# Second projection of an FFN: a join one step later on ScalarE, an update of x one step later on VectorE

## The chip, the cores and the metric

The kernel runs on one core of one Trainium2 chip. The metric is the device time of one execution in microseconds, as a median over runs. Five engines work side by side, each through its own list of instructions in order, and wait for one another through semaphores: TensorE (PE; its weight loads are shown apart as PEld), VectorE (DVE), ScalarE (ACT), GpSimd (POOL) and SyncE (SP), whose queue issues most of the transfers.

## The reference

The kernel computes an encoder trunk of two layers on one sequence of 512 tokens with 1024 channels, in float32. Cut to its frame:

```python
def swiglu(x, w_in, w_out):
    gu = x @ w_in
    g, u = jnp.split(gu, 2, axis=-1)
    return (jax.nn.silu(g) * u) @ w_out

for l in range(DEPTH):                      # DEPTH = 2
    x = x + 0.5 * swiglu(rms_norm(x, ffn1_norm[l]), ffn1_w_in[l], ffn1_w_out[l])
    x = x + mixer(rms_norm(x, mix_norm[l]), ...)
    x = x + 0.5 * swiglu(rms_norm(x, ffn2_norm[l]), ffn2_w_in[l], ffn2_w_out[l])
return rms_norm(x, final_norm)
```

The hidden width of an FFN is 2816. There are four FFN stages, two in each layer, with a mixer (neighbourhood attention and a Fourier mix) between the two of a layer. The change touches the second projection of the four FFN stages, `(silu(g) * u) @ w_out`, and the addition to x that follows it.

## The kernel before

**Products in parts.** Matrix products run in float32r, with each operand split into a high part (ACT copies it into the narrower format) and a low part (DVE subtracts). A product is then three matmuls: high by high, low by high, high by low. A weight comes from memory as `raw` and becomes `whi` (ACT, L191 or L186) and `wlo` (DVE, L194 or L187); some are first added to another block by DVE (`summed`, L164). `whi` and `wlo` have three buffers each. `ws.next()` hands out the next weight and prepares those up to two ahead (`AHEAD`).

**Seven products.** Each large product is a two by two block product done with seven products in the manner of Strassen, numbered 1 to 7. In the second projection the blocks of the result are quarters of x, written `(i, j)`: `i` is the half of the channels, `j` the half of the tokens. Several products serve more than one quarter: product 1 is accumulated in the bank pair `ps[1]`, is subtracted from quarter (0, 0), then product 6 is accumulated on top of it in the same pair (`key = {6: 1, 4: 7}`), and the sum of products 1 and 6 goes into (1, 1), (0, 1) and (1, 0).

**The steps.** The inner dimension is cut in three chunks, `c` = 0, 1, 2. A list of 21 steps (L758 to L769) sets the order on TensorE: steps 0 to 2 are product 1 with chunks 0 to 2, steps 3 to 5 product 2, steps 6 to 17 products 5, 6, 7, 3 for chunk 0, then for chunk 1, then for chunk 2, and steps 18 to 20 product 4. `make(i)` (L772) prepares the activations of step i: some add or subtract two blocks first (`comb`, DVE L750), then ACT splits off the high part (`c1h`, `c2h`, ..., L321) and DVE the low part (`c1l`, `c2l`, ..., L322); the digit is the product. The loop at L920 makes a step's activations one or two steps ahead, issues its matmuls, and then whatever stands behind the step.

**Turned halves.** The activations `silu(g) * u` come out of the first projection with tokens on the partitions and must be transposed. `halves` (L693) has ACT separate the two 16-bit words of each number (`apart`, L341; tiles `zs`) and SP issue a transposing transfer (`zt<-zs`, L347). `joined` (L697) has ACT put the words together again in the tile `at` (L356, two ACT instructions a half here). When the second projection begins, two halves of the last block of four feature tiles are still to be joined: those of the second token half, turned first, and those of the first token half, turned last. `turned.reverse()` at step 2 takes the last one first. It is the block `at[1, 0, 2]`, chunk 2 of product 2, so step 5 is the first to read it. The other is `at[1, 1, 2]`; it is joined behind step 5 and first read for chunk 2 of products 6, 7 and 3.

**Updates of x.** `update(ps, i, j, sign)` (L753) adds a pair of banks to a quarter of x, in two DVE instructions (L756). Where a quarter is done, ACT squares it for the next norm (`squares`, L375), and TensorE transposes it for the next stage (`quad`, L402, matmuls at L413 into `tr`). Behind step 18 quarters (1, 1) and (0, 1) are transposed in three of the four stages; the last stage (`late`) goes on to the final norm instead.

**What sets the order.** TensorE's work, ACT's and DVE's is ordered by a planner when the program is built: it goes by the order in which the program writes the instructions, but lets one pass whose inputs and buffers it reckons ready earlier. Inside a `manual_schedule` block the written order holds for the engines named; the block behind step 18 is one, for DVE and ACT. The planner's reckoning is not the chip's time, so an instruction can stand early in an engine's list and wait there, and all behind it wait too.

Of the kernel before, what the change touches and what calls it, by code (L numbers as in the profile page):

```python
# [90 lines left out]
def encoder_kernel(  # L91
# [19 lines left out]
    def slot(dt=F32, s="k", shape=(4, 256)):  # L111
        return kp.tile([P, *shape], dt, tag="k", name=nm(s), bufs=23)
# [8 lines left out]
    def pair(s="ps"):  # L121
        return [bank(s), bank(s)]
# [149 lines left out]
    class Stream:  # L272
# [32 lines left out]
        def next(self, ahead=AHEAD):  # L305
            self.prep(self.pos + 1 + ahead)
            it = self.items[self.pos]
            self.pos += 1
            return it.out
# [203 lines left out]
    def product(ps, acts, kts, start, stop=True, again=False, hook=None, by_block=False, ahead=AHEAD):  # L513

        h, l, off = acts
        n = (len(kts) + 1) // 2

        def granule(i, w, b):  # L520
            res = []
            for k, kt in enumerate(kts[2 * i : 2 * i + 2]):
                c, z = slice(off + b * P, off + (b + 1) * P), slice(k * T, (k + 1) * T)
                res.append((
                    ps[b], h[:, kt, c], l[:, kt, c], w[0][:, z], w[1][:, z], start and i + k == 0,
                    stop and 2 * i + k == len(kts) - 1,
                ))
            return res

        if by_block:  # L530
            w = [ws.next() for _ in range(n)]
            for b in range(2):
                for i in range(n):
                    late_low(granule(i, w[i], b), again)
            return
        for i in range(n):
            w = ws.next(AHEAD if i < n - 1 and ahead else ahead)
            if i < n - 1:
                late_low(granule(i, w, 0) + granule(i, w, 1), again)
            else:  # L540
                late_low(granule(i, w, 0), again)
                late_low(granule(i, w, 1), again)
            if hook and i == 0:
                hook()
# [70 lines left out]
    def stage_ffn(norm, nxt, late):  # L615
# [81 lines left out]
        def joined():  # L697

            t, j, f0 = turned.pop(0)
            q = 0  # L700
            while q < 4:
                h, c, i = PLACE[f0 + q]
                n = 1
                while q + n < 4 and PLACE[f0 + q + n] == (h, c, i + n):
                    n += 1
                joined_words(at_tile(h, j, c)[:, i : i + n, :], t[:, :, q : q + n, :])
                q += n
# [14 lines left out]
        def settle_at():  # L722
            while late_at:
                to_at(*late_at.pop(0))
# [28 lines left out]
        def update(ps, i, j, sign, bs=(0, 1)):  # L753
            for b in bs:
                v = x[:, 2 * j + b, i * T : (i + 1) * T]
                V.scalar_tensor_tensor(v, ps[b], 0.25 * sign, v, ALU.mult, ALU.add)  # L756
# [15 lines left out]
        def make(i):  # L772
            if i < len(steps) and i not in made:
                m, c, f = steps[i]
                made[i] = hl(f(), c, f"c{m}")
# [144 lines left out]
        for i, (m, c, _) in enumerate(steps):  # L920
            make(i)
            if i:
                make(i + 1)
            key = {6: 1, 4: 7}.get(m, m)
            if key not in ps:
                ps[key] = pair(f"o{key}")
            if m == 4 and c == 0 and nxt.mix:
                make(i + 2)
                ws.finish_stage()
                swap_pools(1)  # L930
            product(
                ps[key], made.pop(i), list(range(len(CHUNK[0][c]))), c == 0 and m in (1, 2, 3, 5, 7), c == 2,
                m in (4, 6), by_block=late and i == len(steps) - 1,
            )
            if i == 0:
                settle_at()
            if i == 2:
                turned.reverse()
                joined()
            if i == 5:  # L940
                joined()
            if m == 4 and c == 0 and not late:
                with tc.manual_schedule(engines={mybir.EngineType.DVE, mybir.EngineType.Activation}):
                    make(i + 2)
                    nxt.quad(1, 1)
                    if nxt.mix:
                        nxt.low01 = nxt.quad_high(0, 1)
                    else:
                        nxt.quad(0, 1)
            make(i + 2)  # L950
            if i == 6 and not late:
                nxt.quad(0, 0)
            if m == 4 and c == 1:
                update(ps[1], 1, 0, 1)
            if m == 4 and c == 0 and late:
                gf[0] = slot(F32, "gf", (D,))
                nc.sync.dma_start(out=gf[0], in_=bass.AP(tensor=gfin.tensor, offset=gfin.offset, ap=[[0, P], [1, D]]))
            if c < 2:
                continue
            if m == 1:  # L960
                update(ps[1], 0, 0, -1)
            elif m == 2:
                update(ps[2], 0, 0, 1)
                nxt.squares(0, 0)
            elif m == 5:
                update(ps[5], 0, 1, 1)
                update(ps[5], 1, 1, -1)
            elif m == 6:
                update(ps[1], 1, 1, 1)
            elif m == 7:  # L970
                update(ps[7], 1, 1, 1)
                nxt.squares(1, 1)
                update(ps[1], 0, 1, -1)
            elif m == 3:
                update(ps[3], 0, 1, 1)
                nxt.squares(0, 1)
                if late:
                    make(i + 3)
            elif late:
                with (  # L980
                    tc.issue_after(ws.items[-1].last.ins),
                    tc.manual_schedule(engines={mybir.EngineType.DVE, mybir.EngineType.Activation}),
                ):
                    ready = nxt.inverses(2)
                    next(ready)
                    gained(2, 0)
                    next(ready)
                    gained(2, 1)
                    for _ in ready:
                        pass  # L990
                    scaled(nxt, 2)
                    update(ps[7], 1, 0, 1, (0,))
                    nxt.squares(1, 0, (0,))
                    root = [nxt.inverse(b, *nxt.terms(b)) for b in range(2)]
                    next(root[0])
                    gained(3, 0)
                    gained(3, 1)
                    scaled(nxt, 3)
                    update(ps[7], 1, 0, 1, (1,))
                    nxt.squares(1, 0, (1,))  # L1000
                    next(root[1])
                    next(root[0])
                    gained(0, 0)
                    next(root[0])
                    gained(0, 1)
                    scaled(nxt, 0)
                    next(root[1])
                    next(root[1])
                    whole(nxt, 1, 0)
                    whole(nxt, 1, 1)  # L1010
            else:
                update(ps[7], 1, 0, 1)
                if not nxt.mix:
                    nxt.squares(1, 0)
                nxt.later((1, 0))
# [8 lines left out]
    def gained(tb, i):  # L1024

        if tb not in ob:
            ob[tb] = slot(F32, "o", (D,))
        o_, v, g, _ = half(tb, i)
        V.tensor_tensor(o_, v, g, ALU.mult)

    def scaled(norm, tb):

        o_, _, _, to = half(tb)
        S.activation(o_, o_, AF.Copy, scale=norm.inv[tb])
        nc.sync.dma_start(out=to, in_=o_)

    def whole(norm, tb, i):
        if tb not in ob:
            ob[tb] = slot(F32, "o", (D,))
        o_, v, g, to = half(tb, i)  # L1040
        V.scalar_tensor_tensor(o_, v, norm.inv[tb], g, ALU.mult, ALU.mult)
        nc.sync.dma_start(out=to, in_=o_)
# [770 lines left out]
    def swap_pools(kind, fetch=True):  # L1813

        if scope[0]:
            scope[0].close()
        scope[0] = ExitStack()
        name = nm("stage")
        scope_pool[0] = scope[0].enter_context(tc.tile_pool(name=name, bufs=1, reuse_waits="tile"))
        if kind:  # L1820
            mix_pool[0] = scope_pool[0]
            raw_pool[0] = mix_raw
        else:
            raw_pool[0] = ffn_raw
        if fetch:
            ws.enter(ws.stage + 1)
# [163 lines left out]
```

## Time and profile before

| | |
|---|---|
| median of 3 runs | 1859.08 us (1858.87 to 1861.8) |
| profiled execution, whole | 1858.25 us |
| its span, first to last instruction | 1856.5 us |
| granted TensorE clock, mean | 0.998 of full speed |
| second projections of the four FFN stages (first step to last) | from about 220, 821, 1143 and 1742 us, some 110 us each |

Busy times and waits stand in the rows that the prediction shows. Times in a timeline are microseconds from the start of the span. A row of the timeline gives start, duration, engine, line, operation and the tiles written and read; in brackets stands how long the engine had idled before it and what ended that. A row of the list of waits reads "engine, tile and line that waited <- what it waited for: total us, number, longest". A TensorE matmul's end is modelled, so the starts of its weight loads (PEld) show best where it stood still.

### The profile page before, as it was taken

What the parts mean: (1) busy time and instruction counts of PE and PEld (TensorE: products, weight loads), DVE (VectorE), ACT (ScalarE), POOL (GpSimd) and SP (SyncE); (2) the same over time, 40 slices, a digit from 0 to 9 for tenths busy, and PEclk for the clock granted to TensorE, in tenths of its full rate; (3) what the DMA queues carried; (4) which work ended last, traced back from release to release, by engine and by line L of the source; (5) the groups of instructions that cost most, each with busy time, mean ns of one, the idle gap of its engine ahead of it and who ended that gap; (6) DMA issues with size and microseconds to landing.
All of it is one profiled execution on the core that took longest, in us unless ns stands there. A gap on an engine that the chain in (4) does not pass through costs nothing.

```text
span 1856.5 us, 24608 instructions
## 1 busy us (share of the span) xinstructions
PE 1842.9 (99%) x8862; PEld 1529.9 (82%) x8862; DVE 1605.1 (86%) x1950; ACT 1311.4 (71%) x1780; POOL 171.4 (9%) x210
## 2 busy tenths in 40 slices
PE   9999999999999999999999999999999999999998
PEld 7888888888888888888788888888888888888886
DVE  7878899786989987889998888998869899888898
ACT  6777875668676767777666777766675776777865
POOL 0001011100111010001010100101001101010010
PEclk9999999999999999999999999999999999999999
DMA  9898798932896788979888887989249867888794
GB/s 302 227 234 220 189 262 271 221 114 91 246 232 180 182 225 221 213 199 260 250 199 220 223 210 207 270 274 215 74 143 237 230 179 174 232 212 209 218 283 146
DMA packets 198458, 394.21 MB, mean 212 GB/s; under 512 B 103808, under 2 KB 103936, under 8 KB 198336
## 3 DMA queue, kind: packets, MB, share of 16 engines
q1 hardware_dynamic: 169664, 294.30, 49.4%
q0 software_dynamic: 28528, 98.33, 29.8%
q8 instruction: 69, 1.13, 0.3%
q14 instruction: 53, 0.43, 0.1%
q10 hardware_dynamic: 144, 0.02, 0.0%
HBM read 365.85 MB, written 2.11 MB: 198 GB/s over the span
## 4 chain that ended last, share of the span: by engine, by line
PE 89%; DVE 5%; issue 2%; DMA 2%; ACT 1%; SPq 0%; DVEq 0%; ACTq 0%
PE A L508 10%; PE A L511 10%; PE A L509 10%; PE B L509 5%; PE B L508 5%; PE B L511 5%; PE o L511 5%; PE o L508 5%; PE o L509 5%; PE ps L315 4%; PE ps L316 3%; PE ps L317 3%; PE C L508 3%; PE C L509 3%; PE C L511 3%
## 5 line engine op out<-in xcount | busy, mean ns | idle before, releaser
L194 DVE TENSOR_TENSOR wlo<-raw,whi 128x1024 fp32r<-128x1024 f32 (+1 forms) x534 | 630.2, 1190 | 165.2 <-ACT whi L191 163.7
L191 ACT ACTIVATE whi<-raw 128x1024 fp32r<-128x1024 f32 (+1 forms) x534 | 545.8, 1033 | 250.9 <-DVE raw L164 57.5
L150 POOL DMA_DIRECT2D raw<-in_wst_dram x166 | 144.3, 886 | 1343.1 <-DMA raw<-in_wst_dram 812.7
L164 DVE TENSOR_TENSOR raw<-raw,raw 128x1024 f32<-128x1024 f32 (+1 forms) x150 | 178.5, 1190 | 2.0
L509 PE MATMUL A<-whi,xl 128*128 128x512 f32 x400 | 155.7, 389 | 0.0
L508 PE MATMUL A<-whi,xh 128*128 128x512 f32 x400 | 155.7, 389 | 0.0
L356 ACT ACTIVATE at<-zt 128x1024 uint16<-128x1024 uint16 (+2 forms) x96 | 110.4, 1167 | 22.4 <-DMA zt<-zs 22.4
L186 ACT ACTIVATE whi<-raw 128x1024 fp32r<-128x1024 f32 (+1 forms) x83 | 86.0, 1036 | 46.6 <-issue 12.5
L511 PE MATMUL A<-wlo,xh 128*128 128x512 f32 x400 | 115.0, 389 | 0.0
L187 DVE SCALAR_TENSOR_TENSOR wlo<-raw,whi 128x1024 fp32r<-128x1024 f32 (+1 forms) x83 | 98.2, 1192 | 11.2 <-ACT whi L186 11.2
L511 PEld LDWEIGHTS A<-wlo,xh 128*128 128x128 f32 x400 | 75.1, 188 | 15.6
L509 PEld LDWEIGHTS A<-whi,xl 128*128 128x128 f32 x400 | 75.1, 188 | 15.4
L508 PEld LDWEIGHTS A<-whi,xh 128*128 128x128 f32 x400 | 75.1, 188 | 15.4
L508 PE MATMUL C<-whi,xh 128*128 128x512 f32 x208 | 81.1, 390 | 0.0
L509 PE MATMUL C<-whi,xl 128*128 128x512 f32 x208 | 81.0, 389 | 0.0
L509 PE MATMUL B<-whi,xl 128*128 128x512 f32 x208 | 81.0, 389 | 0.0
L508 PE MATMUL B<-whi,xh 128*128 128x512 f32 x208 | 80.9, 389 | 0.0
L346 ACT ACTIVATE zs<-th 128x1024 uint16<-128x1024 uint16 x80 | 79.5, 1041 | 0.9 <-DVE th L737 0.9
L730 ACT ACTIVATE th<-sn,rh 128x512 f32<-128x512 f32 x80 | 55.1, 716 | 34.0 <-DVE sn L583 33.0
L578 ACT ACTIVATE sn<-A 128x512 f32<-128x512 f32 x104 | 59.1, 585 | 24.8 <-PE A L511 24.8
L511 PE MATMUL C<-wlo,xh 128*128 128x512 f32 x208 | 59.8, 389 | 0.0
L511 PE MATMUL B<-wlo,xh 128*128 128x512 f32 x208 | 59.8, 389 | 0.0
(438 smaller groups left out, 4680.2 us busy)
## 6 DMA issues: line engine op xcount, KB each, us to landing
raw<-in_wst_dram SPq DMA_DIRECT2D x470, 512.0 KB, 5.7
raw<-in_wst_dram POOLq DMA_DIRECT2D x174, 512.0 KB, 7.8
raw<-in_wst_dram SPq DMA_DIRECT2D x30, 256.0 KB, 4.0
bm<-in_bias_dram SPq DMA_DIRECT2D x16, 384.0 KB, 3.6
x<-in_xin_dram SPq DMA_DIRECT2D x4, 512.0 KB, 10.2
raw<-in_wst_dram POOLq DMA_DIRECT2D x8, 256.0 KB, 9.2
dft<-in_dft_dram POOLq DMA_DIRECT2D x8, 256.0 KB, 4.3
gb<-in_gbias_dram SPq DMA_DIRECT2D x4, 512.0 KB, 15.2
```

The lines of the kernel that those rows point to most:

```text
L150: G.dma_start(out=self.t, in_=wst[GRAN_AT[self.plus]][:, 0 : self.n], accum_op=ALU.add)
L164: V.tensor_tensor(self.raw.t, self.raw.t, self.add.t, ALU.add)
L186: S.activation(hi, t, AF.Copy, scale=-1.0)
L187: self.last = V.scalar_tensor_tensor(lo, t, -1.0, hi.bitcast(F32), ALU.mult, ALU.subtract)
L191: S.activation(hi[:, cs], t[:, cs], AF.Copy)
L194: self.last = V.tensor_tensor(lo[:, cs], t[:, cs], hi[:, cs].bitcast(F32), ALU.subtract)
L315: PE.matmul(ps, lh, rh, start=start, stop=False, skip_group_check=again)
L346: S.activation(s[:, h], words[:, h], AF.Copy)
L356: S.activation(to[:, w], t[:, w], AF.Copy)
L508: PE.matmul(ps, lh, rh, start=start, stop=False, skip_group_check=again)
L509: PE.matmul(ps, ll, rh, start=False, stop=False, skip_group_check=again)
L511: PE.matmul(ps, lh, rl, start=False, stop=stop, skip_group_check=again)
```

## The change

Two pieces of work are written one step later in the loop over the 21 steps; nothing else differs.

- The joining of the last turned half, two ACT instructions in each FFN stage, stood behind step 2 and ahead of `make(4)`. It now stands behind step 3, ahead of `make(5)`. The other half stays behind step 5.
- The update of quarter (0, 1) with the sum of products 1 and 6, two DVE instructions in each FFN stage, stood behind step 16 (product 7, chunk 2), after the update of (1, 1) with product 7. It now stands behind step 17 (product 3, chunk 2), just ahead of the update of the same quarter with product 3.

```diff
@@ -934,7 +934,7 @@
             )
             if i == 0:
                 settle_at()
-            if i == 2:
+            if i == 3:
                 turned.reverse()
                 joined()
             if i == 5:
@@ -970,8 +970,8 @@
             elif m == 7:
                 update(ps[7], 1, 1, 1)
                 nxt.squares(1, 1)
+            elif m == 3:
                 update(ps[1], 0, 1, -1)
-            elif m == 3:
                 update(ps[3], 0, 1, 1)
                 nxt.squares(0, 1)
                 if late:
```

## The prediction

> **What bounds the kernel now.** I read the page's busy times first, then the lists of who waited for whom, then the timeline of each engine at the two places that the diff touches.
>
> ```profile
> span 1856.5 us, 24608 instructions
> PE 1842.9 (99%) x8862; PEld 1529.9 (82%) x8862; DVE 1605.1 (86%) x1950; ACT 1311.4 (71%) x1780; POOL 171.4 (9%) x210
> ```
>
> TensorE sets the time: 1842.9 of 1856.5 us. Anything won must be time in which TensorE stood still, so the list of its weight loads' waits gives the ceiling. The second projection's loads are those that write `o`.
>
> ```profile
> ACT at L356 <- DMA zt<-zs: 22.4, 11, 4.6
> DVE c2l L322 <- ACT c2h L321: 8.3, 4, 2.6
> ...
> PEld o L511 <- DVE wlo L194: 6.6, 17, 1.1
> PEld o L508 <- ACT whi L191: 2.4, 3, 0.9
> ```
>
> The columns are total us, number, longest. In the four second projections together TensorE waits 2.4 us for a high half of a weight (`whi`, made by ACT) and 6.6 us for a low half (`wlo`, made by DVE): 9.0 us, 0.48% of the span, is all that this change can reach. The first two rows hint at a cause: ACT waits for a transposed half to land, and DVE then waits exactly four times for a `c2h`, once for each FFN stage.
>
> ACT in the first FFN stage (start, duration, then in brackets the idle time before and who ended it):
>
> ```profile
> 231.49 1.56 ACT L191 ACTIVATE whi<-raw 128x1024 fp32r<-128x1024 f32 x2
> 235.42 2.57 ACT L356 ACTIVATE at<-zt 128x1024 uint16<-128x1024 uint16 x2 [2.37 <-DMA zt<-zs]
> 237.86 1.03 ACT L321 ACTIVATE c2h<-at 128x1024 fp32r<-128x1024 f32 x1
> 238.80 1.04 ACT L191 ACTIVATE whi<-raw 128x1024 fp32r<-128x1024 f32 x1
> 239.74 1.05 ACT L321 ACTIVATE c2h<-at 128x1024 fp32r<-128x1024 f32 x1
> ```
>
> ACT runs its list in order. It is free at 233.05, idles 2.37 us for the landing, joins for 2.57 us, and only then splits the activations of step 4 (`c2h` at 237.86) and the next weight (238.80). The `c2h` at 237.86 does not read the joined half: step 4 is product 2, chunk 1, and the half joined here is chunk 2, first read by the `c2h` at 239.74 for step 5.
>
> TensorE's loads, and DVE, at the same place:
>
> ```profile
> 238.65 0.19 PEld L509 LDWEIGHTS o<-whi,c2l 128*128 128x128 f32 x1
> 238.87 0.19 PEld L511 LDWEIGHTS o<-wlo,c2h 128*128 128x128 f32 x1
> 239.89 0.19 PEld L508 LDWEIGHTS o<-whi,c2h 128*128 128x128 f32 x1 [0.82 <-ACT whi L191]
> ```
>
> ```profile
> 235.12 1.28 DVE L756 SCALAR_TENSOR_TENSOR x<-o,x 128x512 f32<-128x512 f32 x2
> 238.92 1.23 DVE L322 TENSOR_TENSOR c2l<-at,c2h 128x1024 fp32r<-128x1024 f32 x1 [2.52 <-ACT c2h L321]
> ```
>
> The load at 239.89 starts as the weight split of 238.80 ends (239.84): the stall is the landing's, handed down ACT's list. The other stages show the same on ACT, and two of them on the loads:
>
> ```profile
> 836.01 2.59 ACT L356 ACTIVATE at<-zt 128x1024 uint16<-128x1024 uint16 x2 [3.06 <-DMA zt<-zs]
> 1157.82 2.58 ACT L356 ACTIVATE at<-zt 128x1024 uint16<-128x1024 uint16 x2 [2.20 <-DMA zt<-zs]
> 1755.61 2.58 ACT L356 ACTIVATE at<-zt 128x1024 uint16<-128x1024 uint16 x2 [0.62 <-DMA zt<-zs]
> ```
>
> ```profile
> 840.49 0.19 PEld L508 LDWEIGHTS o<-whi,c2h 128*128 128x128 f32 x1 [0.93 <-ACT whi L191]
> 1162.29 0.19 PEld L508 LDWEIGHTS o<-whi,c2h 128*128 128x128 f32 x1 [0.67 <-ACT whi L191]
> ```
>
> 0.82 + 0.93 + 0.67 = 2.42 us: the whole 2.4 us row. The last FFN stage, with 0.62 us of idle, has no such stall.
>
> **Edit 1, the join a step later.** Two ACT instructions in each of four stages change place: eight of 1.3 us (2.57 / 2). Nothing is added or removed, and no transfer is issued by them. `c2h` of step 4, which reads nothing of the half, goes ahead of them and fills the idle 2.37 us from 233.05 on (1.03 us of work). What then stands behind the wait is the join, at most the next weight split, and `c2h` of step 5.
>
> At the least, then, ACT's list after the join moves up by one `c2h`, 238.80 - 237.86 = 0.94 us. The weight split ends at 238.90 and the load of step 4 could follow its predecessor (238.87) at the usual 0.23 us. 0.94 covers each of 0.82, 0.93 and 0.67, so the first term is 2.4 us. At the most the weight split also goes ahead of the join, once TensorE has left its buffer, and ACT gains the whole idle time. What is late next would be `c2h` of step 5: at worst it waits for the landing at 235.42, a join of 2.57 and a split or two, 240 at the latest, as now. Step 5 begins 24 loads of 0.23 us after 239.1, at 244.6, so it stays covered by step 4; without that cover it would cost up to the 2.4 us that it replaces.
>
> The second term comes through DVE. Its 2.52 us of idle before `c2l` is the last that it has for a long time, and its weight work then runs behind: the 6.6 us row. `c2l` of step 4 could run at 236.4, but the next low halves need ACT's high halves, which come 0.94 us earlier at the least and up to 2.4 at the most. TensorE itself is some 0.8 us earlier. DVE's gain against TensorE is therefore 0.1 us (0.94 - 0.8) to 1.6 us (2.4 - 0.8) in each of three stages, taken out of the 6.6 us. I take 0.7, a little under the middle of 0.85, since weight buffers still tie DVE to TensorE: 3 x 0.7 = 2.1 us. The last stage, with 0.62 us of idle, is set at nothing. Ends: 0.3 and 4.8 us.
>
> On the size of the first term:
>
> ```profile
> 233.00:252.00 19.00, 18.60 (x82) 14.91 (x81) 16.48 (x18) 14.42 (x17) 3.50 (x4) 1.00 1.02 239
> 833.00:853.00 20.00, 19.50 (x86) 15.65 (x85) 17.37 (x19) 14.76 (x16) 2.33 (x3) 1.00 0.90 217
> 1155.00:1175.00 20.00, 19.76 (x87) 15.89 (x86) 17.64 (x20) 15.58 (x18) 2.20 (x3) 1.00 0.91 224
> ```
>
> After length come PE and PEld busy. By matmul busy time only 0.40 + 0.50 + 0.24 = 1.14 us is idle here. The Trainium skill ("Perfetto Trace Analysis", section "Identifying the Most-Contended Engine") says that matmul busy time is a poor measure of what is left, and that weight loads tell more; by it the term is 2.4 us, and by the matmul rows 1.1. This trace sides with the page: the load at 239.89 comes 1.02 us after 238.87, against 0.23 us between undisturbed ones.
>
> **Edit 2, the update of x a step later.** Two DVE instructions in each of four stages change place. DVE at the end of the first stage, TensorE's loads, and two ACT rows:
>
> ```profile
> 308.25 1.21 DVE L194 TENSOR_TENSOR wlo<-raw,whi 128x1024 fp32r<-128x1024 f32 x1
> ...
> 311.39 2.47 DVE L756 SCALAR_TENSOR_TENSOR x<-o,x 128x512 f32<-128x512 f32 x4
> 313.79 1.81 DVE L194 TENSOR_TENSOR wlo<-raw,whi 128x1024 fp32r<-128x1024 f32 x2
> 315.52 1.21 DVE L322 TENSOR_TENSOR c4l<-at,c4h 128x1024 fp32r<-128x1024 f32 x1
> 316.66 1.27 DVE L756 SCALAR_TENSOR_TENSOR x<-o,x 128x512 f32<-128x512 f32 x2
> ```
>
> ```profile
> 309.52 0.77 PEld L511 LDWEIGHTS o<-wlo,c3h 128*128 128x128 f32 x4 [1.06 <-DVE wlo L194]
> ...
> 317.35 1.89 PEld L413 LDWEIGHTS tr<-ident,x 128*128 128x128 f32 x16
> ```
>
> ```profile
> 310.36 1.05 ACT L321 ACTIVATE c4h<-at 128x1024 fp32r<-128x1024 f32 x1
> 311.31 0.61 ACT L191 ACTIVATE whi<-raw 128x512 fp32r<-128x512 f32 x1
> ```
>
> Four updates stand together at 311.39: two with product 7, then the two that move. The stall of 1.06 us at 309.52 lies before them and waits for the low half of 308.25, so the move cannot remove it. Moved, they stand ahead of the updates at 316.66, which need product 3. The two low halves and `c4l` between come 1.2 us earlier. Their inputs are there (`whi` by 311.92, `c4h` by 311.41), so DVE does not idle, and the updates at 316.66 still end at 317.93. That matters: the 16 transposes at 317.35 read x, and the second eight, from 318.3, need just those updates; the slack is 0.4 us. TensorE shows no wait for what comes earlier. I take 0; the ends are a gain of 1.2 us in the one stage where the 1.06 us stall would otherwise slide down here, and a loss of 1.2 us in each stage if DVE does idle there.
>
> **Sum.** 2.4 + 2.1 + 0 = 4.5 us. The profiled execution took 1858.25 us, 1.75 outside its span, and would take 1853.75. The median of the three runs, 1859.08, is 0.83 above it: forecast 1859.1 - 4.5 = 1854.6 us.
>
> **Rivals.**
>
> *DVE gives nothing back* (0.22). The `whi` stalls go, but DVE stays tied to TensorE through the three weight buffers: 0.3 instead of 2.1 us. For it: ACT's list moves by little more than TensorE does. Against: DVE loses 2.52 us of idle. 1859.1 - 2.7 = 1856.4 us.
>
> *All idle time is won* (0.10). The weight split goes ahead of the join too: 2.4 + 4.8 = 7.2 us, 1851.9 us.
>
> *The edit doesn't do what it says* (0.08). The order on ACT is a planner's, not the program's; it may put the join ahead of the same `c2h` as now, or ACT may not have waited for the transfer at all. 1859.1 us. Against the second:
>
> ```profile
> 229.47 3.93 SPq L347 DMA_TRANSPOSE zt<-zs  x1
> ```
>
> ```profile
> DMA to landing us min/median/max: 4.3/5.5/8.8
> ```
>
> The first row is the half's issue on SP's queue, the second covers all 44 transposing transfers: 5.5 us after 229.47 is 235.0, past ACT's 233.05.
>
> By the Trainium skill ("DMA: Bandwidth & Descriptors", section "Latency and other measured facts"), such a transfer runs at 261 GB/s; the 524,288 bytes of one half would take an estimated 2.0 us, landing at 231.5, before ACT is free, with edit 1 worth nothing. The trace disagrees: 4.3 us is its fastest.
>
> *The moved update lands on the transposes* (0.12). If the planner leaves DVE idle where the updates stood, x is ready 1.2 us later, the second eight transposes wait, and so does ACT's squaring with the weight splits behind it. At 1.2 us in each of four stages this costs 4.8 us; it decides from 0.4 us of idle on. For it: the window
>
> ```profile
> 295.00:322.00 27.00, 26.36 (x123) 21.17 (x122) 27.00 (x31) 16.47 (x23) 2.25 (x3) 1.00 0.85 265
> ```
>
> has DVE (third busy time) busy for 27.00 of 27.00 us, so what is late there stays late. Against: the same row, which leaves no idle for it to come from. With edit 1 yielding nothing, 1863.9 us; with its 2.4 us, 1861.5.
>
> **How the numbers follow.** The forecast has 0.48, with a range of its own from 1853.3 to 1855.9 (the second term between 0.8 and 3.4 us). A difference of 0.2%, 3.7 us, is about what a measurement of this kernel can tell from no change; faster by more means under 1855.4. That holds for most of the forecast (0.44), all of the case with all idle time, and a little of the first rival (0.03): 0.57. Slower by more means over 1862.8, the last rival without help from edit 1: 0.07. The rest, 0.36, is within 0.2%. The range runs from 1851.8, about half of the best case, to 1859.6, which leaves out the slower one.
>
> **What would show it.** In the changed kernel's trace: `c2h` of step 4 right after the two weight splits, with no idle before it; the row of `c2l` waiting for `c2h` down from 8.3 to under 2 us; the 2.4 us row gone; the 6.6 us row at 4 to 5 us. At the stage's end two updates where four stood, four just before the transposes, and no wait of a `tr` load. The forecast is wrong if the join still precedes that `c2h`, if the 6.6 us row grows, or if `tr` loads wait.

## The result, and the profile after

The median went from 1858.97 us (1856.97 to 1863.28, 18 runs) to 1856.13 us (1853.62 to 1859.59, 18 runs). The medians differ by 2.8 us, where 4.5 were forecast. The ratio is 0.9982, with a 95% interval of 0.9976 to 0.9988, which is 3.3 us (2.2 to 4.5). The profiled execution took 1856.45 us, 1.80 less than the one before.

The busy times of the changed kernel:

```profile
span 1854.7 us, 24607 instructions
PE 1841.4 (99%) x8862; PEld 1530.4 (83%) x8862; DVE 1605.3 (87%) x1950; ACT 1311.6 (71%) x1780; POOL 171.5 (9%) x210
```

Each engine in this row has as many instructions as before, and its busy time differs by 1.5 us at most; the span is 1.8 us shorter. From the changed kernel's list of waits, the rows that answer to those of before:

```profile
ACT at L356 <- DMA zt<-zs: 19.0, 8, 3.3
...
PEld o L511 <- DVE wlo L194: 6.0, 13, 1.1
...
PEld o L508 <- ACT whi L191: 0.3, 1, 0.3
```

Waits for a high half fell from 2.4 to 0.3 us. Waits for a low half fell only from 6.6 to 6.0. The row in which `c2l` waited for `c2h` (8.3 us before) is no longer in the list. ACT in the first FFN stage, in the second, and the join of the third (start, duration, and in brackets the idle time before):

```profile
231.61 1.56 ACT L191 ACTIVATE whi<-raw 128x1024 fp32r<-128x1024 f32 x2
233.08 1.05 ACT L321 ACTIVATE c2h<-at 128x1024 fp32r<-128x1024 f32 x1
235.11 1.06 ACT L191 ACTIVATE whi<-raw 128x1024 fp32r<-128x1024 f32 x1 [0.98 <-PE o L509]
236.08 2.57 ACT L356 ACTIVATE at<-zt 128x1024 uint16<-128x1024 uint16 x2
238.51 1.03 ACT L191 ACTIVATE whi<-raw 128x1024 fp32r<-128x1024 f32 x1
...
829.00 1.04 ACT L321 ACTIVATE c2h<-at 128x1024 fp32r<-128x1024 f32 x1
829.95 0.61 ACT L191 ACTIVATE whi<-raw 128x512 fp32r<-128x512 f32 x1
833.86 2.58 ACT L356 ACTIVATE at<-zt 128x1024 uint16<-128x1024 uint16 x2 [3.30 <-DMA zt<-zs]
836.31 1.03 ACT L191 ACTIVATE whi<-raw 128x1024 fp32r<-128x1024 f32 x1
...
1157.02 2.59 ACT L356 ACTIVATE at<-zt 128x1024 uint16<-128x1024 uint16 x2 [1.08 <-DMA zt<-zs]
```

The planner made two different lists for ACT out of one edit. In the first stage (the third and the last have the same order) not only `c2h` of step 4 but also the next weight split went ahead of the join; ACT's only idle time there is 0.98 us, for a weight buffer that TensorE still read. In the second stage the join still stands ahead of that weight split, which waits out the landing behind it. That is where the last wait for a high half is:

```profile
837.39 0.19 PEld L508 LDWEIGHTS o<-whi,c2h 128*128 128x128 f32 x1 [0.25 <-ACT whi L191]
```

DVE at the same place, in stages one, two, three and the last:

```profile
239.57 1.23 DVE L194 TENSOR_TENSOR wlo<-raw,whi 128x1024 fp32r<-128x1024 f32 x1 [0.78 <-ACT whi L191]
...
837.38 1.23 DVE L194 TENSOR_TENSOR wlo<-raw,whi 128x1024 fp32r<-128x1024 f32 x1 [1.76 <-ACT whi L191]
...
1160.54 1.23 DVE L194 TENSOR_TENSOR wlo<-raw,whi 128x1024 fp32r<-128x1024 f32 x1 [1.99 <-ACT whi L191]
...
1758.38 1.22 DVE L194 TENSOR_TENSOR wlo<-raw,whi 128x1024 fp32r<-128x1024 f32 x1 [0.79 <-ACT whi L191]
```

The waits for `c2h` did not vanish, they became shorter waits for `whi`. Before, DVE idled here for 2.52 us in the first stage, and in the second and third for these times:

```profile
839.53 1.22 DVE L322 TENSOR_TENSOR c2l<-at,c2h 128x1024 fp32r<-128x1024 f32 x1 [2.63 <-ACT c2h L321]
...
1161.33 1.23 DVE L322 TENSOR_TENSOR c2l<-at,c2h 128x1024 fp32r<-128x1024 f32 x1 [2.35 <-ACT c2h L321]
```

So DVE won 2.52 - 0.78 = 1.74 us in the first stage, 0.87 in the second and 0.36 in the third. TensorE itself won 0.82, 0.93 - 0.25 = 0.68 and 0.67 us there. Against TensorE, DVE is ahead by 0.92, 0.19 and -0.31 us at this place.

DVE has a second idle time later, in step 12, where it waits for another weight's `whi`. In the second stage, before and then after:

```profile
881.88 1.23 DVE L194 TENSOR_TENSOR wlo<-raw,whi 128x1024 fp32r<-128x1024 f32 x1 [1.59 <-ACT whi L191]
```

```profile
879.19 1.23 DVE L194 TENSOR_TENSOR wlo<-raw,whi 128x1024 fp32r<-128x1024 f32 x1 [2.01 <-ACT whi L191]
```

ACT waited 3.10 and then 3.52 us there for the weight to land. So the second stage lost again 0.42 of the 0.87 us that DVE had won.

The next table carries this to the stages. Weight loads within one product follow one another at 0.227 us; what a gap has beyond that is counted as standstill, except 0.99 us in step 7 of the first three stages, where eight transposes stand between the loads. Length is from the first load of step 0 to the first of step 18.

| stage | length before, us | after | standstill in steps 6 to 17, before | after |
|---|---|---|---|---|
| first | 93.2 | 90.7 | 1.99 | 0.06 |
| second | 93.8 | 93.5 | 2.78 | 3.42 |
| third | 91.8 | 91.5 | 0.76 | 1.10 |
| last | 90.1 | 89.8 | 0.45 | 0.07 |

Stage one won 2.5 us, the three others 0.2 to 0.3 each. This is one execution before and one after, and a stage varies between executions (see the runs with edit 1 alone and without the early preparation below). After step 18 the last stage shows a stall that the profile of before does not have:

```profile
1835.72 0.77 PEld L511 LDWEIGHTS o<-wlo,c4h 128*128 128x128 f32 x4 [1.08 <-DVE wlo L194]
```

At the end of the first stage DVE's list reads as the second edit wrote it, two updates, then the low halves and `c4l`, then four updates:

```profile
308.96 1.28 DVE L756 SCALAR_TENSOR_TENSOR x<-o,x 128x512 f32<-128x512 f32 x2
310.16 1.82 DVE L194 TENSOR_TENSOR wlo<-raw,whi 128x1024 fp32r<-128x1024 f32 x2
311.89 1.22 DVE L322 TENSOR_TENSOR c4l<-at,c4h 128x1024 fp32r<-128x1024 f32 x1
313.03 2.48 DVE L756 SCALAR_TENSOR_TENSOR x<-o,x 128x512 f32<-128x512 f32 x4
```

```profile
314.98 1.89 PEld L413 LDWEIGHTS tr<-ident,x 128*128 128x128 f32 x16
```

The 16 transposes follow at 314.98 without a wait.

### The profile page after: what moved, and what is told of

Same layout as the page of the kernel before. It is cut to its first block, busy times and chain, and to the rows that moved or that the text cites. A ratio compares the mean times of both kernels' runs of the same rounds, so it can differ in the third digit from the quotient of the medians.

```text
span 1854.7 us, 24607 instructions
## 1 busy us (share of the span) xinstructions
PE 1841.4 (99%) x8862; PEld 1530.4 (83%) x8862; DVE 1605.3 (87%) x1950; ACT 1311.6 (71%) x1780; POOL 171.5 (9%) x210
## 4 chain that ended last, share of the span: by engine, by line
PE 92%; DVE 4%; DMA 2%; issue 1%; ACT 1%; SPq 0%; DVEq 0%; POOL 0%; ACTq 0%; POOLq 0%
PE A L508 10%; PE A L511 10%; PE A L509 10%; PE o L511 6%; PE o L508 6%; PE o L509 6%; PE B L509 5%; PE B L508 5%; PE B L511 5%; PE ps L315 4%; PE ps L316 3%; PE ps L317 3%; PE C L508 3%; PE C L509 3%; PE C L511 3%
```

## The experiments

Every ratio is against the kernel before, with both kernels run on the same chip (7 to 11 runs of the kernel in question, 21 to 33 of the one before). The questions were these: which edit carries the time (the expectations call it Theory A that edit 1 carries all of it); whether the place of the next weight split against the join decides what edit 1 is worth (Theory C); and what the stalls that are left wait for.

### One edit at a time

Edit 1 alone (run e1) is the change without this part of it (a diff from the changed kernel):

```diff
                 nxt.squares(1, 1)
-            elif m == 3:
                 update(ps[1], 0, 1, -1)
+            elif m == 3:
                 update(ps[3], 0, 1, 1)
```

> Edit 1 alone: the join a step later, the update of x where it was. Theory A (the join does it all, the moved update fills a place where TensorE does not wait): 2.5 to 3 us faster than before, as the changed kernel, ratio about 0.9985; the four stages' TensorE stalls as in the changed kernel, with the stall of 1.0 us in the last stage too. Theory B (the two edits need one another): less than half of that, ratio 0.9993 or above.

1856.68 against 1859.73 us, ratio 0.9982 (0.9973 to 0.9991). ACT's list is that of the changed kernel. In this profile the half of the third stage landed in time, and that stage is 90.7 us long instead of 91.5; the second is 92.5 instead of 93.5. The last, from its first load to its last, is 106.2 us, against 105.5 with the change and 104.8 before. The row of low halves stands at 4.5 us.

Edit 2 alone (run e2) puts the join back; ACT's list is then that of before:

```diff
-            if i == 3:
+            if i == 2:
                 turned.reverse()
                 joined()
```

> Edit 2 alone: the update of x a step later, the join where it was. Theory A: no difference from before, ratio 1.0000 within 0.0005, with the three waits of TensorE for a high half (2.4 us together) all there. Theory B: at least 1 us faster, ratio 0.9995 or below. If the moved update falls on the transposes or on the final norm, slower by 1 us or more, with a wait of a tr load or a longer way from the last product to the end.

1859.75 against 1859.73 us, ratio 1.0001 (0.9992 to 1.001). Its list of waits:

```profile
PEld o L511 <- DVE wlo L194: 6.5, 17, 1.1
...
PEld o L508 <- ACT whi L191: 3.8, 3, 2.3
```

Edit 1 alone has the whole ratio of the change, edit 2 alone none. The rival that gives edit 2 a share has no support within 0.1%, which is what the intervals allow. The waits for a high half stand in the kernel with the old join (3.8 us) and not in the one with the new (0.3 in edit 1 alone). They are larger than the 2.4 of before by one row of the second stage:

```profile
837.09 2.58 ACT L356 ACTIVATE at<-zt 128x1024 uint16<-128x1024 uint16 x2 [4.49 <-DMA zt<-zs]
...
841.56 0.19 PEld L508 LDWEIGHTS o<-whi,c2h 128*128 128x128 f32 x1 [2.35 <-ACT whi L191]
```

With the join in the old place ACT waited 4.49 us for the half in this execution, against 3.06 in the profile before, and TensorE 2.35 against 0.93. The transfer of this half is issued 9.3 us after the stage's first load in both, and took 6.1 us to land in the profile of before and 7.6 here. What the old order costs depends on when the half lands, and that varies between executions.

### Where the join stands against the weight split

The first kernel (run e4) pins the join behind the next weight split in every stage, which alters the lists of ACT and DVE in the second stage alone. `issue_after` forbids the planner to put an instruction ahead of the named one. Diff from the changed kernel:

```diff
-                    S.activation(hi[:, cs], t[:, cs], AF.Copy)
+                    self.first = S.activation(hi[:, cs], t[:, cs], AF.Copy)
...
             if i == 3:
                 turned.reverse()
-                joined()
+                with tc.issue_after(ws.items[ws.prepped - 2].first.ins):
+                    joined()
```

> Both edits, and the join pinned behind the next weight split on ACT; the list of ACT changes in the second FFN stage alone, where the planner had put the join ahead of that split. Theory C (what a stage gains is decided by whether the weight split passes the join): the second stage's TensorE stalls fall from 3.6 us to under 1.5, as in the first stage, and the whole is some 2 us faster than the changed kernel, ratio to before about 0.9975. Theory D (DVE is bound by its own work there): the 0.2 us before step 4 goes and the later stalls stay above 3 us, ratio 0.9984 as the changed kernel.

1853.98 against 1859.73 us, ratio 0.9972 (0.9961 to 0.9984). ACT in its second stage:

```profile
830.16 0.61 ACT L191 ACTIVATE whi<-raw 128x512 fp32r<-128x512 f32 x1
833.27 1.07 ACT L191 ACTIVATE whi<-raw 128x1024 fp32r<-128x1024 f32 x1 [2.50 <-PE o L509]
834.24 2.58 ACT L356 ACTIVATE at<-zt 128x1024 uint16<-128x1024 uint16 x2
```

ACT still idles 2.50 us, but now for TensorE to leave a weight buffer, and the half has landed meanwhile. The second stage is 90.9 us long instead of 93.5 and stands still for 0.36 us. The second idle time of DVE, in step 12 of this stage, fell from 2.01 to 0.51 us as well. The weight waited for is brought by a transfer that GpSimd issues: 46.8 to 47.2 us after the stage's first load in the five kernels whose join stands behind the weight split there, 47.6 to 49.9 in the eight others. It lands 9.4 to 11.6 us after that. The list of waits of this kernel:

```profile
PEld o L511 <- DVE wlo L194: 1.7, 4, 0.9
```

The interval overlaps that of the change. But runs e7 and e10 below differ by this pin alone too, 0.9986 and 0.9975, and all four kernels with this pin (e4, e9, e10 and e11, 0.9971 to 0.9975) are ahead of all five with the changed kernel's join (0.9982 to 0.9986).

The opposite pin (run e5), the join ahead of the weight split in every stage (`joined` hands back its last ACT instruction for it):

```diff
+            with tc.issue_after(joined_last[0].ins) if i == 3 else nullcontext():
+                product(
...
-            if i == 3:
+            if i == 2:
+                make(4)
                 turned.reverse()
-                joined()
+                joined_last.append(joined())
```

> Both edits, with the join pinned ahead of the next weight split on ACT in all four stages, as the planner has it in the second alone. The split of the step's activations still passes the join. Theory C: the first stage loses its gain after step 5 and shows 1.5 to 2 us of waits for low halves again; the whole is 1.5 to 2.5 us slower than the changed kernel, ratio to before 0.9993 to 1.0. Theory D: no difference from the changed kernel, ratio 0.9985.

1857.93 against 1859.73 us, ratio 0.999 (0.9982 to 0.9999). The first stage, 90.7 us long with the changed kernel, is 92.2 here, with 1.90 us of standstill in products 5 to 7. ACT at the join:

```profile
232.95 1.05 ACT L321 ACTIVATE c2h<-at 128x1024 fp32r<-128x1024 f32 x1
235.62 2.59 ACT L356 ACTIVATE at<-zt 128x1024 uint16<-128x1024 uint16 x2 [1.62 <-DMA zt<-zs]
238.07 1.98 ACT L191 ACTIVATE whi<-raw 128x1024 fp32r<-128x1024 f32 x2
```

By the ratios, `c2h` alone ahead of the join is worth 0.1%, and 0.28% with the weight split ahead too (the intervals overlap a little). But this pin is not a clean test: the planner also wrote the lists of ACT and DVE anew from step 7 on in the first and the third stage. The first stage's standstill begins at step 11 only, behind two other weights, for which ACT waited 1.73 and 1.86 us. The third stage, with the same lists, had no stall: its half landed 4.3 us after the issue, and ACT waited neither for it nor for those weights. So the loss of the first stage is not shown to be the pin's.

The last of this group (run e12) pins the join behind the second weight split, to see how late it may stand (`ws.prepped - 1` for `- 2`):

> e4 with the join pinned behind the second weight split too, so that the activations of step 5 are split about 1 us later. If step 4 covers them, as the prediction has it, TensorE shows no wait for c2h or c2l and the time is that of e4 within 1 us. If the join was needed that early, TensorE waits at the start of step 5 and the kernel is 1 us or more slower than e4.

1857.32 against 1858.77 us, ratio 0.9993 (0.9984 to 1.0002): nearly all of the gain is gone. No load waits in step 5, so its activations are still made in time, yet the kernel is not within 1 us of the first one of this group, as was expected for that case. Its list of waits has

```profile
PEld o L511 <- DVE wlo L194: 5.2, 10, 1.1
```

of which 4.7 us (1.90 in products 5 to 7, 1.67 in product 3, 1.11 in product 4) fall into the last stage. They follow two weights that landed late: ACT waited 2.88 and 1.85 us for them in steps 11 and 12, and DVE idled 1.75 and 1.49 us behind ACT. Runs e7 and e10 below, which don't have this pin, show the same there (1.92 and 1.42 us on DVE in e10). In nine kernels (the changed one, e1, e4 and e6 to e11) the lists of ACT and DVE are one and the same in the last stage up to step 15, and steps 6 to 15 stood still for 0 to 1.9 us in them. So this stall varies between executions, and this part of the loss needs no second weight split ahead of the join. Another 2 us of this profile, against that of e4, lie outside the second projections, and the planner wrote the lists of ACT and DVE anew in all stages, so the kernel does not show how late the join may stand.

### The stalls that are left

In the second stage the stall at product 3's last step waits for a low half behind two updates of x and a weight sum. First the load, then DVE, in the changed kernel:

```profile
907.90 0.76 PEld L511 LDWEIGHTS o<-wlo,c3h 128*128 128x128 f32 x4 [1.10 <-DVE wlo L194]
```

```profile
904.30 1.28 DVE L756 SCALAR_TENSOR_TENSOR x<-o,x 128x512 f32<-128x512 f32 x2
905.50 1.22 DVE L164 TENSOR_TENSOR raw<-raw,raw 128x1024 f32<-128x1024 f32 x1
906.63 1.22 DVE L194 TENSOR_TENSOR wlo<-raw,whi 128x1024 fp32r<-128x1024 f32 x1
```

So the other update with the sum of products 1 and 6, of quarter (1, 1), was moved a step later as well, first together with both edits (run e7):

```diff
             elif m == 6:
-                update(ps[1], 1, 1, 1)
+                pass
             elif m == 7:
+                update(ps[1], 1, 1, 1)
                 update(ps[7], 1, 1, 1)
```

> The changed kernel, with the other update by the sum of products 1 and 6, that of quarter (1, 1), a step later too: from behind step 15 to behind step 16. It stands ahead of the low half that step 17 waits for. If these two instructions are what makes it late, the waits in step 17 (1.64 us in the second stage, 0.38 in the third) fall under 0.5 us each, and the kernel is about 1 us faster than the changed one, ratio to before 0.9975 to 0.998. If DVE is late there by more than they take, the stall stays or moves to step 18.

1854.98 against 1858.67 us, ratio 0.9986 (0.9977 to 0.9994). The stall went as it was meant to, from 1.64 to 0.13 us in the second stage and from 0.38 to 0 in the third, but the ratio is no better than the change's. In this profile a `tr` load of the second stage then waited 0.5 us for an update of x, the rival that the prediction had for edit 2, and the last stage stood still for 2.3 us in steps 12 to 16, behind two late weights. The same with the update of (0, 1) in its old place (run e8), so that six updates stand together:

> The join a step later, the update of (1, 1) a step later as in e7, and that of (0, 1) back in its old place, so that six updates stand together behind step 16. If edit 2 is worth something as room for the other update, the low halves for step 18 come 1.2 us later than in e7 and TensorE waits for them at step 18, up to 1 us in each stage: ratio to before 0.9982 or above, 1 to 3 us slower than e7. If the place has slack to spare, it equals e7.

1855.31 against 1858.67 us, ratio 0.9986 (0.9978 to 0.9995). Here the stall reappears one step down, 1.14 us at step 18 of the second stage and 0.17 in the first. The loss of 1 to 3 us against the kernel above that was expected with it did not come. Edit 2's place is worth nothing in this company either.

The stall at step 19 of the last stage has four updates and a subtraction ahead of it on DVE:

```profile
1830.92 2.48 DVE L756 SCALAR_TENSOR_TENSOR x<-o,x 128x512 f32<-128x512 f32 x4
1833.32 1.22 DVE L750 TENSOR_TENSOR at<-at,at 128x1024 f32<-128x1024 f32 x1
1834.45 2.36 DVE L194 TENSOR_TENSOR wlo<-raw,whi 128x1024 fp32r<-128x1024 f32 x2
```

The subtraction belongs to step 20, which the last stage prepares early (`if late: make(i + 3)`). Taking that early preparation out of the changed kernel (run e6):

> The changed kernel without the early preparation of step 20 in the last stage: that preparation then stands behind the low halves of the weights for step 19. If the stall of 1.0 us at step 19 comes from the subtraction of step 20 standing ahead of those low halves on DVE, it goes, and the kernel is 0.5 to 1 us faster than the changed one, ratio to before about 0.998 or a little below. If step 20 then comes late instead, a stall of up to 1 us appears there and nothing is won.

1855.26 against 1858.67 us, ratio 0.9984 (0.9976 to 0.9993): nothing won. In its first three stages the lists are those of the changed kernel; they are 90.7, 93.2 and 90.7 us long. The wait moved to step 20, where a load waits 1.84 us for the low half of the activations, `c4l`. With the pinned join and both updates moved as well (run e9, all three edits on top of the change):

> e4, e6 and e7 together: the join behind the next weight split in all stages, both updates later, step 20 of the last stage not prepared early. If the gains add up, TensorE's waits in the four second projections fall from the 6.3 us of the changed kernel to under 1 us; 4 to 6 us faster than the changed kernel, ratio to before 0.9955 to 0.9965. If DVE's loads of weights set the pace after all, no better than e4, 0.9972.

1853.0 against 1858.67 us, ratio 0.9975 (0.9966 to 0.9984). All stalls of the first three stages are gone (90.7 us each), and only a wait of 1.7 us for `c4l` remains. The 4 to 6 us over the changed kernel that were expected if the gains add up did not come; the ratio is that of the pinned join alone, within the intervals. The pinned join and both updates, with the early preparation kept (run e10):

> e4 and e7 together, without e6, whose early step was needed: both updates later, the join behind the next weight split in all stages, the last stage's early preparation of step 20 kept. TensorE's waits in the four second projections: 1 to 1.5 us, all in the last stage at step 19, against 6.3 in the changed kernel. 4 to 5 us faster than the changed kernel, ratio to before about 0.997, and about 0.5 us faster than e9.

1854.12 against 1858.77 us, ratio 0.9975 (0.9965 to 0.9985). Again three stages at 90.7 us, and 2.15 + 1.15 us of standstill in the last, behind late weights in steps 12 to 16 (0.41 of it for a high half) and at step 19. Expected were 0.5 us less than in e9, and the median is 1.1 us more, with the same ratio. On top of it (run e11), the updates and squares of (0, 1) in the last stage were put behind step 18, after the preparation of steps 19 and 20:

```diff
             if m == 4 and c == 0 and late:
+                last_of_01()
                 gf[0] = slot(F32, "gf", (D,))
...
             elif m == 3:
-                update(ps[1], 0, 1, -1)
-                update(ps[3], 0, 1, 1)
-                nxt.squares(0, 1)
                 if late:
                     make(i + 3)
+                else:
+                    last_of_01()
```

`last_of_01()` holds the three lines taken out.

> e10, and in the last stage both updates of quarter (0, 1) and its squares behind step 18 instead of step 17. If the four updates ahead of the low halves for step 19 are what makes these late, the stall of about 1 us at step 19 goes: 0.5 to 1 us faster than e10. If the final norm then waits for that quarter, the end comes later by as much and nothing is won.

1852.92 against 1858.77 us, ratio 0.9971 (0.996 to 0.9981). The waits of this kernel's weight loads have no row that writes `o`: no product of the second projections waits any more. One of the transposes behind step 18 does, in the first stage:

```profile
PEld tr L413 <- DVE x L756: 0.3, 1, 0.3
```

In median it is the fastest of the kernels run, though its interval overlaps those of the change and of the pinned join alone. Its edit accounts for the 1.15 us at step 19; the 2.15 us in steps 12 to 16 went because the weights landed earlier in this execution (ACT waited 0.80 and 1.83 us there, against 3.05 and 1.76). Per stage, the parts (pinned join; pinned join with both updates; this one) leave 1.7, 3.5 and 0 us of waits in one profile each, so the order of the first two is not to be read from them.

## Why the prediction was right or wrong

**The first term, 2.4 us, was right.** The waits for a high half went from 2.4 to 0.3 us; edit 1 alone did it. What the step described "at the least", `c2h` alone ahead of the join, is the second stage; what it described "at the most", the weight split ahead too, is what the other stages have.

**The second term, 2.1 us, failed.** It set DVE's gain against TensorE at 0.7 us in each of three stages and so the row of low halves at 4 to 5 us. In its place the waits on DVE at the join give 0.92, 0.19 and -0.31 us, 0.8 in sum, and the row stands at 6.0, 0.6 lower. That is near the low end, 0.3, of its bounds. The gain was not a size per stage: in these two profiles the first stage won nearly all that it had (1.99 to 0.06 us), while standstill grew in the second (2.78 to 3.42) and in the third (0.76 to 1.10).

In the second stage the planner left the weight split behind the join, so the low half that follows waited out 1.76 us of the landing, and 0.42 us more were lost in step 12 to a weight that landed late; the term had no place for that second wait. Pinning the join behind the split took the stage from 93.5 to 90.9 us, with a ratio of 0.9972. In the third stage the list is the good one, but the half took 7.8 us from issue to landing (5.9 in the profile of before), so ACT waited 1.08 us for it at 1157.02 and the following weight's low half waited 1.99 us. That is bad luck of this execution: in e1 and e6, with the same list, the half took 6.1 us, ACT did not wait for it, and the stage stood still for 0.15 and 0 us. The second stage stood still for 2.0 and 3.2 us in them, and for 0 to 0.36 in the four kernels with the pin, so its miss lies in the order.

**The last stage, set at nothing, got a new wait.** From its first load to its last it took 105.5 us, 0.7 more than before. Its waits of low halves went from 0.45 us in the middle to 0.07, and 1.08 came at step 19. DVE's waits for a high half in the middle of that stage, and the place of `c5l`, in the profile of before and then in that of after, with ACT's row:

```profile
1795.26 1.22 DVE L322 TENSOR_TENSOR c5l<-at,c5h 128x1024 fp32r<-128x1024 f32 x1
...
1800.29 1.22 DVE L194 TENSOR_TENSOR wlo<-raw,whi 128x1024 fp32r<-128x1024 f32 x1 [0.41 <-ACT whi L191]
```

```profile
1797.41 1.22 DVE L194 TENSOR_TENSOR wlo<-raw,whi 128x1024 fp32r<-128x1024 f32 x1 [1.43 <-ACT whi L191]
...
1800.82 1.22 DVE L322 TENSOR_TENSOR c5l<-at,c5h 128x1024 fp32r<-128x1024 f32 x1
...
1796.32 2.01 ACT L191 ACTIVATE whi<-raw 128x1024 fp32r<-128x1024 f32 x2 [1.78 <-DMA raw<-in_wst_dram]
```

DVE idled 1.43 - 0.41 = 1.02 us more there, and TensorE stood still for 0.38 less: 1.4 us of DVE's lead. The weight itself was no later, since its split began 57.2 us after the stage's first load before and 57.3 after. But the planner had moved `c5l`, 1.2 us of work, from ahead of this low half to behind it, some 40 us after the join that the edit moved. What the lead was at step 19, in the profile of before, DVE first and then the load:

```profile
1836.19 2.35 DVE L194 TENSOR_TENSOR wlo<-raw,whi 128x1024 fp32r<-128x1024 f32 x2
```

```profile
1837.94 0.87 PEld L511 LDWEIGHTS o<-wlo,c4h 128*128 128x128 f32 x4
```

The first of the two low halves ended at 1837.4 (half of the pair), 0.6 us ahead of its load. Less 1.4 that is a wait of about 0.8, and 1.08 was measured. Edit 1 alone, which has the changed kernel's list here, shows this wait (1.15 us). So does edit 2 alone (1.1 us), with the list of before, in an execution in which that low half began 1.6 us later in the stage. So a late weight brings the wait without the new list, and whether the kernel before shows it in other executions is open, since it has one profile.

**Edit 2 at nothing was right**, by the run with it alone (1.0001) and by the rows: DVE's order is the one forecast, DVE does not idle where the updates stood, and no `tr` load waits. The rival in which the moved update lands on the transposes falls with that for this change; with the second update moved too, in e7, one `tr` load did wait 0.5 us.

**Of the other rivals**, the one in which DVE gives nothing back (0.3 us for the second term) is the nearest in time, 1856.4 us against 1856.13 measured, and nearest in the row of low halves (6.6 to 6.0). It is not true of every stage, since the first gave back 1.93 us. The measured median lies 0.2 us above the forecast's own range, which ended at 1855.9, and a gain of more than 0.2%, which had a chance of 0.57, did not come. All idle time won, at 1851.9 us, is close to the kernels in which the planner's order was overruled (1852.92 with no wait left, with both updates moved too); it needed a written order, which the change does not have. That ACT did not wait for the transfer at all falls with the old order's rows: ACT's wait of 3.06 us came up again, as 4.49, when edit 2 stood alone. The figure of 261 GB/s for such a transfer (the Trainium skill, "DMA: Bandwidth & Descriptors", section "Latency and other measured facts") is a rate, and the estimate of 2.0 us from it covers the bytes alone. It was no measure of the landing, which took 4.3 us at the least from issue; no run here tests the rate itself.

**What the sum comes to.** By the two rows of waits, 2.4 - 0.3 = 2.1 us and 6.6 - 6.0 = 0.6 us were won, 2.7 together; the medians show 2.8 and the ratio 3.3. The one profiled execution is only 1.8 us shorter, and stages of one order differ by about 1 us between profiles, so the agreement of this sum is in part luck.

**What stays open**: why the weights of the last stage are late in some executions and not in others, how much of the loss with the join behind two weight splits is the pin's, and whether the two places of the updates differ at all (0.9986 both).

## What to carry to other kernels

On an engine that runs its list in order, an instruction that waits for a transfer also delays everything written behind it, and the loss shows up on engines that never touch the transferred data; look for what behind the wait does not need it, and count the instructions that go ahead, not only the one moved. A planner decides stage by stage, so read each stage's list after the edit: three stages took the weight split ahead and one did not, and pinning that one gave 0.9972 against 0.9982, with intervals that overlap. Compare the whole lists before calling an edit or a pin a clean test, since the planner also moved work some 40 us behind the place that was edited. A gain passed on from one engine to the next is not to be credited per stage at its mean, since it counts only as far as the next wait that ends on TensorE.

## What the runs showed of the hardware

The landing of the same transposing transfer varied by more than a microsecond from execution to execution. In the second stage it took 6.1 us from issue to landing in the profile of before and 7.6 with edit 2 alone, with the same order on ACT and the issue at the same place of the stage; ACT waited 3.06 and 4.49 us for it. In the third stage it took 7.8 us in the changed kernel and 6.1 with edit 1 alone. Where ACT no longer waited for the transfer it waited for TensorE to release one of the three weight buffers, for 0.98 us in the first stage of the changed kernel and 2.50 us in the second of the pinned one, and no load of step 4 or 5 waited there.
